# Two half heads of attention probabilities turned by VectorE blocks and a DRAM round trip, and the sample rows' averaging later in the order

## The chip, the cores and the metric

The kernel runs on one core of a Trainium2 chip. It has five engines with a queue of instructions each: PE (TensorE, matrix products and transposes), DVE (VectorE), ACT (ScalarE), POOL (GpSimd) and SP (SyncE, which here only issues DMAs). The metric is the device time of one execution in microseconds (us), the median over the runs.

## The reference

One layer of a hybrid decoder, for a prompt of 512 tokens and 8 running sequences with one new token each (the sample rows), d_model 1024, in float32. What this case touches is mixer B, the dilated window attention of the prompt, and the layer norm of the sample rows at the end:

```
for window, dil in ((128, 1), (512, 4), (2048, 16)):       # mixer B, 8 heads of 64
    dist = arange(window // dil + 1) * dil;  idx = q_idx[:, None] - dist     # rows < 0 are masked
    logits = einsum('bqhd,bqjhd->bhqj', q, k[idx]) * 64**-0.5 + rel_bias[t5_bucket(dist)].T
    m = max(logits);  p = exp(logits - m);  s = sum(p)
    outs += [einsum('bhqj,bqjhd->bhqd', p, v[idx]) / s]
o_b = sum(w * o) / sum(w),  w = s * exp(m - max over the three m)
...
mix = concat([o_a * silu(ga), o_b * silu(gb)])             # o_a: gated linear attention, 4 heads
y = mix @ w_out                                            # 1024 x 1024
x_new = layer_norm(2**0.25 * x + y, ln_g, ln_b)            # for the prompt's and for the sample rows
```

## The kernel before

All work of the step is one program for one core. The input projection goes by column groups (`ps_qa`, `ps_ka`, `ps_qb`, ... are PSUM tiles of these groups); matrices are split into a high and a low part (`hi_`, `lo_`), and each product is the sum of three matmuls. Then come both mixers, and at the end the output projection: `ps_y` matmuls by row pairs of the prompt, whose result VectorE adds to `y`, followed by the layer norm.

**The order of the work.** Every stage is a generator, a task, that yields one instruction after another. A planner (class `Plan`) issues them: the table `TIMES` (L241) has a due time for each step of each task, and the planner always takes the task whose next step is due first (`run`). Each engine executes its instructions in the order in which they were issued, so the table sets the order on every engine; the times in it are not waits. A trailing `a` in the table picks the second of two engines where a step offers two (VectorE or ScalarE). All instructions are recorded under the one line that issues them, L677 (L679 in the changed kernel). `QUEUE` says for each round trip through DRAM which engine issues its DMAs: `G` is POOL, `D` is SyncE.

**Softmax and values of the prompt.** The queries come in four blocks of 128, two to a half (`pi` 0 and 1). `softmax(h, q, ...)` (L1650) takes the scores of head `h` and block `q` from PSUM, adds the bias strip, takes the exponential (ScalarE) and the sum, and normalises into `pr`. The keys that are far away are folded in a tile `far`. The rest of `pr` is turned: TensorE transposes its 128x128 blocks into a bank `ps_pt`, and VectorE or ScalarE copies them into `pt`, which holds two heads (tile `pt21` is the second half of heads 4 and 5). `weighted(g, pi)` (L1696) waits for four heads and multiplies `far` and `pt` by the values `vp` and `v` into `ps_pv`, as one batch of matmuls, first all of `far`, then `pt` by heads. `weighted(1, 1)` takes the second half of heads 4 to 7.

**Turning through DRAM.** Other tiles are turned in another way already. `blocks` (L1046) transposes inside each 32x32 block on VectorE, `store_blocks` (L1051) writes the result to a scratch tensor in DRAM, and `load_turned` (L1055) reads it back with the blocks exchanged, in pieces of 32 numbers, 128 bytes. `ysc` and `yx` are such a pair for a part of the output, `vsc` for values, `osc` for mixer A.

**The sample rows at the end.** `residual_sample` (L2209) turns the sample rows' output (`ps_ys`), adds it to `w_s`, sums over the row (`sums_s`), averages over the row's parts by a small matmul with a matrix `avg` into `ps_ms` (the mean), subtracts, squares, and averages again into `ps_vs` (the variance):

```
        yield V.tensor_reduce(sums[:, 0:1], y, axis=AX.X, op=ALU.add)
        ps = yield bank("t", "ps_ms")
        yield T.matmul(ps[:ROWS, 0:1], avg, sums_s[:, 0:1], start=True, stop=True)
        yield V.tensor_copy(sums[:, 0:1], ps[:64, 0:1])
```

These small matmuls stand on TensorE in the middle of the `ps_y` matmuls of the output projection. `early_mean` and `last_norm` finish the last row pair. SyncE issues nearly all DMAs in one order: weights, the cached keys (`past`) and values (`vv`, each with its factors `pb`) of the eight running sequences, the bias strips, and the stores.

Of the kernel before, what the change touches and what calls it, by code (L numbers as in the profile page):

```python
# [21 lines left out]
P = 128  # L22
# [58 lines left out]
QUEUE = dict(y="G", v="D", k="G", o="D", a="D")  # L81
SLOW, SHARE = 1100, 1.7

# [159 lines left out]
first_loads 302 1 1 1 1 1 1 1 1225 2286 187 794 1 1 1 1 1 1 1 1 1 1 10481 3044 1  # L243
# [36 lines left out]
softmax|0|0|ps_s00|pr00 71199 352 723 534a 940 514  # L280
softmax|0|1|ps_s00|pr00 71401 533a 745 449 1793 109 494a
softmax|1|0|ps_s10|pr10 71736 689 659 455 3680 286a
sample_logit|0|past0|qbc0 71782 167 1786 6 1787 1980
# [16 lines left out]
evac_f|ps_vb0_f1|1 83824a 2706 -191 588 8171  # L300
# [18 lines left out]
sample_softmax 103293 726 338a 3854 19 473 80 1533 3 8495 4537 119 119 97 553 136 1206 475 400 292 -77 1473 1161 80263  # L319
keys_out|ps_kb3_1|3|1 103292  # L320
keys_store|1 105547 1358 1 1303 1 1940 159 8
sample_logit|7|past7|qbc7 110333 4933 1 2304 1239 1586
evac|ps_gb0_0|0 106220 693 17 1176a 104
evac|ps_gb0_1|1 108107 1 1 1
evac_f|ps_vb1_f0|0 118480a 439a 9948
values_store|0 117568
evac_f|ps_vb1_f1|1 115262a 6000a 3961 1 8209
values_turn|0 117569 1 1239 2
sample_v|vnt|vnt|out_7_dram 117565 1a 1
# [4 lines left out]
evac|ps_gb1_0|0 129481 642 617 872 78  # L334
scores|1|1 124376 397
# [15 lines left out]
softmax|5|0|ps_s50|pr50 134486 1252 896 64a 6389 6
softmax|5|1|ps_s50|pr50 134834 1383 483 427a 7587 1 670a
weighted|0|1 136602 2460a 1250a
softmax|6|0|ps_s60|pr60 140937 392 657 608a 2788 5a
softmax|6|1|ps_s60|pr60 143973 1 333 1 3333 405 341a
softmax|7|0|ps_s70|pr70 144973 1 2463 547a 1685 335a
evac_f|ps_va0_f1|1 144565a 47a 584 1126 6000 599
values_store|1 146916
softmax|7|1|ps_s70|pr70 146915 725 1213 354a 867 776 695a
mix_b|1|0 149500 500 1500  # L360
mix_b|1|1 151500 500 1500
evac|ps_va0_2|2 149776
values_turn|1 156714 986 1100 979
sample_value|2|vv2|pb2 157706 359 738 1975 2787
evac|ps_va0_3|3 151292a
scores|2|1 150934 1089
softmax|5|2|ps_s52|pr52 154303 952 1152 1752a 2622 2104 1869 1 5a
# [3 lines left out]
softmax|5|3|ps_s53|pr53 154696 1263 753 1641 4028 733 1642 1a 4a  # L371
sample_value|3|vv3|pb3 164764 974 1104 519 4664
evac|ps_gb2_0|0 156601 109 643 338 4
evac|ps_gb2_1|1 158795 6 975 1001
scores|3|1 164789 1
softmax|6|2|ps_s62|pr62 165736 1619 1519 494a 682 521 2064 798 232
sample_value|4|vv4|pb4 175659 3 1724 613 3989
softmax|6|3|ps_s63|pr63 166837 1902 793 190 1063 299 4436 1 1a
softmax|7|2|ps_s72|pr72 165733 1100 525 249a 2540 249 38 138 391
evac_f|ps_va1_f0|0 165732 1 411 3 886a  # L380
softmax|7|3|ps_s73|pr73 167352 2344 699 690a 8 2024 1707 1 371a
sample_value|5|vv5|pb5 184671 1 10 1 5285
# [12 lines left out]
sample_value|7|vv7|pb7 195635 1 4315 111 3631
gla_head|0|0 188890 1 240 242 534 1 2628a 245a 265a 590a
gla_head|0|1 191991 1 1 1 2528 72 4128a 1a 1a 490a
evac|ps_gb3_1|1 185463
mix_b|1|3 199537 4796 1
evac|ps_ga0_0|0 193940 250  # L400
# [281 lines left out]
def trunk(ctx: ExitStack, tc: tile.TileContext, xT, xp, xs, state, ck, cv, w_in, wab, gnorm,  # L682
# [95 lines left out]
    B = {}  # L778
# [1634 lines left out]
```

## Time and profile before

| | |
|---|---|
| runs shown | 274.9, 276.59, 277.6 us; median 276.59 |
| profiled execution, its own time | 273.72 us |
| its span | 271.9 us |
| TensorE, matmul | 262.8 us busy, 97% |
| VectorE | 217.6 us, 80% |
| ScalarE | 152.5 us, 56% |
| POOL | 72.9 us, 27% |
| the queue of SyncE's DMAs | 75.9% of 16 DMA engines' time, 56.69 MB |

The span goes from the first to the last instruction of the profiled execution; what lies around it makes the rest of its own time. Busy shares are averages over the whole span; the stages have different limits, so what an edit is worth is read at its own place. An engine named in brackets behind a row is what ended the idle time before that row.

### The profile page before, as it was taken

How to read it: one execution, taken by the hardware profiler on the slowest of the kernel's cores; microseconds unless marked ns; L12 is line 12 of the kernel's file. 1: busy time of each engine (PE TensorE's matmuls, PEld its weight loads, DVE VectorE, ACT ScalarE, POOL GpSimd, SP SyncE). 2: the span in 40 equal slices, each digit the busy share in tenths (PEclk: the TensorE clock that was granted, in tenths of full speed). 3: DMA queues.
4: the chain of work that ended last, by engine and by line, in shares of the span. 5: the costliest groups of instructions: out<-in, count | busy, mean ns of one | idle time of the engine just before them, and what ended most of it. 6: DMA issues, size and time to landing. Idle time of an engine off the chain costs nothing.

```text
span 271.9 us, 7336 instructions
## 1 busy us (share of the span) xinstructions
PE 262.8 (97%) x2831; PEld 246.2 (91%) x2831; DVE 217.6 (80%) x542; ACT 152.5 (56%) x450; POOL 72.9 (27%) x92
## 2 busy tenths in 40 slices
PE   8999999999999999999999999999999999997990
PEld 4999999999999999999989899989999999985890
DVE  4753889999999999486985888976798996429895
ACT  4754766665647393436874785654859456104511
POOL 3000000000263945810054153454753001420200
PEclk9999999999999999999999999999999999997997
DMA  7995698255998899959999996998799899993132
GB/s 221 348 250 120 170 284 232 69 136 161 309 304 174 273 272 216 241 158 272 278 188 283 318 199 192 287 308 257 231 216 236 233 230 259 314 206 83 77 154 82
DMA packets 79215, 60.10 MB, mean 221 GB/s; under 512 B 28453, under 2 KB 69995, under 8 KB 79181
## 3 DMA queue, kind: packets, MB, share of 16 engines
q1 hardware_dynamic: 77981, 56.69, 75.9%
q0 software_dynamic: 768, 2.62, 4.1%
q8 instruction: 22, 0.36, 0.6%
q10 hardware_dynamic: 432, 0.33, 0.4%
q14 instruction: 12, 0.10, 0.1%
HBM read 49.62 MB, written 10.80 MB: 222 GB/s over the span
## 4 chain that ended last, share of the span: by engine, by line
PE 69%; DVE 12%; DMA 11%; ACT 4%; issue 2%; SPq 1%; DVEq 0%; ACTq 0%; POOLq 0%
PE ps_qb L677 9%; PE ps_kb L677 9%; PE ps_gb L677 7%; PE ps_y L677 6%; PE ps_ka L677 5%; PE ps_vb_f L677 4%; PE ps_vb L677 4%; PE ps_qa L677 4%; PE ps_ga L677 4%; DMA y<-in_xp_dram 4%; DMA yx<-ysc 3%; PE ps_va L677 2%; PE ps_pv L677 2%; PE ps_va_f L677 2%; PE ps_l L677 2%; DMA vv<-in_cv_dram 2%
## 5 line engine op out<-in xcount | busy, mean ns | idle before, releaser
L677 POOL TENSOR_TENSOR past<-past,qbc 128x256 f32<-128x256 f32 x32 | 26.3, 854 | 80.6 <-DMA qbc<-qsd 73.9
L677 POOL TENSOR_TENSOR vv<-vv,pb 128x256 f32<-128x256 f32 x32 | 26.9, 872 | 51.9 <-DMA pb<-psd_s 27.9
L677 ACT ACTIVATE pr<-pr,ms 128x128 f32<-128x128 f32 (+3 forms) x52 | 24.7, 492 | 14.7 <-DVE ms L677 14.6
L677 PE MATMUL ps_ka<-xx,hi_ka 128*128 128x264 f32 (+1 forms) x64 | 12.7, 294 | 0.1
L677 DVE CUSTOM_DVE_ANT_0 pr<-ps_s,strip 128x128 f32<-128x128 f32 (+3 forms) x32 | 11.9, 407 | 0.8 <-DMA strip<-tabx 0.5
L677 ACT ACTIVATE d<-d 128x512 f32<-128x512 f32 x11 | 6.8, 643 | 10.0 <-DVE d L677 10.0
L677 ACT COPY pt<-ps_pt 128x256 f32<-128x256 f32 (+1 forms) x23 | 7.6, 348 | 8.3 <-PE ps_pt L677 8.3
L677 PE MATMUL ps_pt<-cf,pr 128*128 128x128 f32 x56 | 11.0, 278 | 0.1
L677 PEld LDWEIGHTS ps_ka<-xx,hi_ka 128*128 128x128 f32 x64 | 10.2, 197 | 0.9 <-ACT hi_ka L677 0.9
L677 DVE TENSOR_REDUCE lt<-past 128x8 f32<-128x512 f32 x16 | 10.4, 672 | 0.0
L677 DVE TENSOR_REDUCE o_pv<-vv 128x4 f32<-128x1024 f32 x8 | 9.7, 1206 | 0.0
L677 POOL DMA_DIRECT2D ysc<-yw x3 | 2.3, 782 | 25.3 <-DVE yw L677 25.3
L677 PE MATMUL ps_ka<-xx,lo_ka 128*128 128x264 f32 (+1 forms) x32 | 8.9, 291 | 0.0
L677 DVE SCALAR_TENSOR_TENSOR y<-y,yx 128x256 f32<-128x256 f32 x6 | 2.4, 414 | 7.7 <-DMA yx<-ysc 7.7
L677 PEld LDWEIGHTS ps_pt<-cf,pr 128*128 128x128 f32 x56 | 6.6, 140 | 1.1 <-ACT pr L677 0.5
L677 ACT ACTIVATE qh<-ps_qb 128x128 fp32r<-128x128 f32 x16 | 5.2, 436 | 3.3 <-PE ps_qb L677 3.3
L677 PE MATMUL ps_pv<-pt,v 128*64 128x128 f32 (+1 forms) x80 | 6.9, 318 | 0.0
L677 PE MATMUL ps_s<-kp,qh 64*128 64x256 f32 (+1 forms) x64 | 6.8, 302 | 0.0
L677 DVE TENSOR_TENSOR d<-b 128x1024 f32<-128x1024 f32 (+1 forms) x6 | 6.8, 1130 | 0.0
L677 DVE RECIPROCAL ms<-ms 128x1 f32<-128x1 f32 x32 | 4.4, 153 | 2.8 <-ACT pr L677 2.7
L677 DVE STREAM_TRANSPOSE yw<-feat_y 128x256 f32<-128x256 f32 x6 | 3.6, 626 | 3.7 <-ACT feat_y L677 3.7
L677 ACT COPY feat_y<-ps_yf 128x256 f32<-128x256 f32 x8 | 2.9, 368 | 6.5 <-PE ps_yf L677 6.5
(566 smaller groups left out, 1075.0 us busy)
## 6 DMA issues: line engine op xcount, KB each, us to landing
past<-in_ck_dram SPq DMA_DIRECT2D x8, 512.0 KB, 5.4
vv<-in_cv_dram SPq DMA_DIRECT2D x8, 512.0 KB, 7.0
pb<-psd_s SPq DMA_DIRECT2D x8, 512.0 KB, 9.0
s<-in_state_dram SPq DMA_DIRECT2D x4, 512.0 KB, 5.5
qbc<-qsd SPq DMA_DIRECT2D x8, 256.0 KB, 4.7
y<-in_xp_dram SPq DMA_DIRECT2D x4, 512.0 KB, 3.5
x_raw<-in_xT_dram SPq DMA_DIRECT2D x6, 260.0 KB, 5.6
out_dram<-y SPq DMA_DIRECT2D x3, 512.0 KB, 2.6
```

Source lines behind the costliest of these rows:

```text
L677: getattr(eng.eng, op.fn)(*op.args, **op.kw)
```

## The change

Three things change.

First, a list `BY_DRAM` names two halves of heads: head 0 first half, head 5 second half. Their `pr` is turned by VectorE's 32x32 block transposes straight into `pt`, and when both query blocks of the half are there, the tile is stored into a scratch tensor `psc` in DRAM (192 KB for head 0, 256 KB for head 5) and loaded back into the same place, turned (1536 and 2048 pieces of 128 bytes). Both DMAs are issued by SyncE. Seven TensorE transposes (three of head 0, four of head 5) and their four copies out of PSUM are left out; four block transposes, two stores and two loads are new.

Second, `residual_sample` gets later due times from its `sums_s` on.

Third, the rest of the table of due times is written anew in many places, so that neighbours change places on all engines but POOL, whose order stays as it was. Among these, four ScalarE steps `s<-s,a_s` stand earlier.

```diff
-QUEUE = dict(y="G", v="D", k="G", o="D", a="D")
+QUEUE = dict(y="G", v="D", k="G", o="D", a="D", p="D")
+BY_DRAM = [(0, 0), (5, 1)]
...
-softmax|5|2|ps_s52|pr52 154303 952 1152 1752a 2622 2104 1869 1 5a
-softmax|5|3|ps_s53|pr53 154696 1263 753 1641 4028 733 1642 1a 4a
+softmax|5|2|ps_s52|pr52 154303 952 1152 1752a 2622 2104 218
+softmax|5|3|ps_s53|pr53 154696 1263 753 1641 4028 733 335 530 6430
...
-residual_sample 214696 1 840 507 26537 906 2067 2101 343 181 346 2398 1 1 1364 10028 717 353
+residual_sample 214696 1 840 507 26537 2919 1500 5000 200 200 600 4000 300 300 300 3600 1000 400
...
+    psc = {(h, pi): scratch(f"psc{h}{pi}", 3 + pi) for h, pi in BY_DRAM}
...
+        nk = (n - far) // P
+        if (h, pi) in BY_DRAM:
+            w = B[f"pt{h // 2}{pi}"][:, h % 2, :(3 + pi) * P].rearrange("p (k q) -> p k q", q=P)
+            yield blocks(w[:, j * (1 + pi):j * (1 + pi) + nk], pr[:, far:n])
+            free(pr_all)
+            mark(f"pw{h}{pi}")
+            if plan.marks[f"pw{h}{pi}"] == 2:
+                yield store_blocks(queue["p"], psc[h, pi], w)
+                yield load_turned(queue["p"], w.rearrange("p k (a j) -> p (k a) j", j=32), psc[h, pi])
+                for _ in range(2):
+                    mark(f"p{h}{pi}")
+            return
         pt = yield bank("t", f"ps_pt{h}{q}")
-        nk = (n - far) // P
         for k in range(nk):
             yield T.transpose(pt[:, k * P:k * P + P], pr[:, far + k * P:far + k * P + P], ident)
```

Three places in the order. On TensorE the mean of the sample rows, before (`mhb`, `mlb` are parts of the mixed features of mixer B, `mha`, `mla` of mixer A, `hi_wo` and `lo_wo` the output weights; numbers are buffer numbers):

```order
L677 MATMUL ps_y_3981<-hi_wo__3499,mla_3662 128x512
L677 MATMUL ps_y_4030<-hi_wo__3551,mhb_2138 128x512
L677 MATMUL ps_y_4030<-lo_wo__3552,mhb_2138 128x512
L677 MATMUL ps_y_4030<-hi_wo__3551,mlb_2139 128x512
L677 MATMUL ps_ms<-sums_s,avg 66x1
L677 MATMUL ps_y_4030<-hi_wo__3551,mhb_2138 128x512
L677 MATMUL ps_y_4030<-lo_wo__3552,mhb_2138 128x512
```

and in the changed kernel:

```order
L679 MATMUL ps_y_4025<-hi_wo__3726,mha_3660 128x512
L679 MATMUL ps_y_4025<-lo_wo__3727,mha_3660 128x512
L679 MATMUL ps_y_4025<-hi_wo__3726,mla_3661 128x512
L679 MATMUL ps_ms<-sums_s,avg 66x1
L679 MATMUL ps_y_4025<-hi_wo__3726,mha_3660 128x512
L679 MATMUL ps_y_4025<-lo_wo__3727,mha_3660 128x512
L679 MATMUL ps_y_4025<-hi_wo__3726,mla_3661 128x512
L679 MATMUL ps_y_4086<-hi_wo__3549,mhb_2134 128x512
```

Before, three matmuls of this `ps_y` tile stood ahead of `ps_ms`, now all but the last three do: `ps_ms` has moved 18 matmuls later, and `ps_vs`, which was 16 instructions behind it, now stands 23 behind.

On SyncE the stretch of the fifth and sixth `vv` (buffers `vv4`, `vv5`), before, with the semaphores that each DMA waits for (DMAHW are earlier DMAs of the ring):

```order
L677 DMA vv4_2778<-in_cv_dram 128x1024 [waits DMAHW0_49,Pool_49]
L677 DMA pb4_2853<-psd_s_95 128x1x1024 [waits DMAHW1_49,DVE_49]
L677 DMA raw0_ga2__2870<-in_w_in_dram 128x8x128 [waits DMAHW2_49,Activation_49]
L677 DMA raw0_ga3__2883<-in_w_in_dram 128x8x128 [waits DMAHW3_49,Activation_49]
L677 DMA vv5_2928<-in_cv_dram 128x1024 [waits DMAHW4_49,Pool_49]
L677 DMA pb5_2963<-psd_s_95 128x1x1024 [waits DMAHW5_49,DVE_49]
```

and in the changed kernel:

```order
L679 DMA vv4_2778<-in_cv_dram 128x1024 [waits DMAHW2_49,Pool_49]
L679 DMA psc51_104<-pt21_2756 128x4x128 [waits DMAHW3_49,DVE_49]
L679 DMA pb4_2847<-psd_s_95 128x1x1024 [waits DMAHW4_49,DVE_49]
L679 DMA raw0_ga2__2864<-in_w_in_dram 128x8x128 [waits DMAHW5_49,Activation_49]
L679 DMA raw0_ga3__2877<-in_w_in_dram 128x8x128 [waits DMAHW6_49,Activation_49]
L679 DMA vv5_2922<-in_cv_dram 128x1024 [waits DMAHW7_49,Pool_49]
L679 DMA pt21_2756<-psc51_104 128x16x32 [waits DMAHW3_49,DMAHW0_49,PE_49]
L679 DMA pb5_2958<-psd_s_95 128x1x1024 [waits DMAHW1_49,DVE_49]
```

Head 5's store has come between `vv4` and `pb4`, and its load between `vv5` and `pb5`. Head 0's store and load stand much earlier on SyncE, the load right ahead of the store `vsc<-vbw` of the first values.

On ScalarE the squares of the second `ps_oa` (mixer A's output; `s` is the running state of the sequences), before:

```order
L677 CAST hi_wo__3450<-raw_wo__3292 128x512 x2
L677 ACTIVATE sq,ssq<-ps_oa_3397 128x128
L677 ACTIVATE sq,ssq<-ps_oa_3398 128x128
L677 ACTIVATE sq,ssq<-ps_oa_3397 128x128
L677 ACTIVATE sq,ssq<-ps_oa_3398 128x128
L677 ACTIVATE s_3269<-s_3269,a_s 128x128 x4
L677 ACTIVATE sq,ssq<-ps_oa_3397 128x128
```

and in the changed kernel:

```order
L679 ACTIVATE oa_3029<-ps_oa_3163,rmss 128x128
L679 ACTIVATE s_3264<-s_3264,a_s 128x128 x4
L679 CAST hi_wo__3450<-raw_wo__3284 128x512 x2
L679 ACTIVATE sq,ssq<-ps_oa_3397 128x128
L679 ACTIVATE sq,ssq<-ps_oa_3398 128x128
```

The four `s<-s,a_s` stood in the middle of the squares and now stand ahead of them and of the two casts. On VectorE, head 5's two block transposes stand ahead of the reduction `o_pv<-vv` and of the copy `feat<-ps_va_f`.

More of the change, by code (lines that the diff above doesn't have):

```diff
@@ L279 @@
 keys_out|ps_kb0_1|0|1 73438
-softmax|0|0|ps_s00|pr00 71199 352 723 534a 940 514
-softmax|0|1|ps_s00|pr00 71401 533a 745 449 1793 109 494a
+softmax|0|0|ps_s00|pr00 70260 352 723 534a 802
+softmax|0|1|ps_s00|pr00 71401 533a 745 449a 6000 1435 5055
 softmax|1|0|ps_s10|pr10 71736 689 659 455 3680 286a
-sample_logit|0|past0|qbc0 71782 167 1786 6 1787 1980
+sample_logit|0|past0|qbc0 71778 1 1 1 3747 1980
 softmax|1|1|ps_s10|pr10 71938 1191 602 8 3763 1 6a
@@ L318 @@
 evac|ps_kb3_1|1 103284 7
-sample_softmax 103293 726 338a 3854 19 473 80 1533 3 8495 4537 119 119 97 553 136 1206 475 400 292 -77 1473 1161 80263
 keys_out|ps_kb3_1|3|1 103292
-keys_store|1 105547 1358 1 1303 1 1940 159 8
-sample_logit|7|past7|qbc7 110333 4933 1 2304 1239 1586
+sample_softmax 107106 1 1a 1101 21 473 80 1533 3 8495 4389 267 119 97 553 136 1206 475 400 292 -77 1473 1161 81937
+sample_logit|5|past5|qbc5 98500 3187 1 1 3857 1388
 evac|ps_gb0_0|0 106220 693 17 1176a 104
+keys_store|1 106424 481 1 1303 1 1940 159 8
 evac|ps_gb0_1|1 108107 1 1 1
+sample_logit|6|past6|qbc6 110190 1 16 1 7240 1
+sample_logit|7|past7|qbc7 110333 4933 1 2304 1443 1382
 evac_f|ps_vb1_f0|0 118480a 439a 9948
+evac_f|ps_vb1_f1|1 118479a 6000a 3961 1 8209
+sample_v|vnt|vnt|out_7_dram 117565 1a 1
 values_store|0 117568
-evac_f|ps_vb1_f1|1 115262a 6000a 3961 1 8209
 values_turn|0 117569 1 1239 2
-sample_v|vnt|vnt|out_7_dram 117565 1a 1
 evac|ps_vb1_2|2 118812a
@@ L333 @@
 sample_values 126150 4645 -308 1121 10667 2825 3358 717 13578 2296 5229 2031 8031 2620 6193 2570
-evac|ps_gb1_0|0 129481 642 617 872 78
-scores|1|1 124376 397
+evac|ps_gb1_0|0 130591 642 617 872 78
+scores|1|1 123466 397
+mix_b|0|0 125209 646 10841
+mix_b|0|1 131386 1660 2329
 softmax|2|2|ps_s22|pr22 126804 562 961 514 641 474 780 1 531
@@ L356 @@
 softmax|7|0|ps_s70|pr70 144973 1 2463 547a 1685 335a
+softmax|7|1|ps_s70|pr70 146915 725 1213 354a 867 776 695a
 evac_f|ps_va0_f1|1 144565a 47a 584 1126 6000 599
-values_store|1 146916
-softmax|7|1|ps_s70|pr70 146915 725 1213 354a 867 776 695a
 mix_b|1|0 149500 500 1500
 mix_b|1|1 151500 500 1500
+values_store|1 146916
+values_turn|1 156714 986 1100 979
 evac|ps_va0_2|2 149776
-values_turn|1 156714 986 1100 979
 sample_value|2|vv2|pb2 157706 359 738 1975 2787
+scores|2|1 150934 1089
 evac|ps_va0_3|3 151292a
-scores|2|1 150934 1089
-softmax|5|2|ps_s52|pr52 154303 952 1152 1752a 2622 2104 1869 1 5a
+sample_value|3|vv3|pb3 161850 3888 1104 519 4664a
 softmax|4|2|ps_s42|pr42 152536 287 1 224 7724 1 1 1 335
@@ L392 @@
+evac|ps_va1_3|3 178179a
 evac|ps_gb3_0|0 183537 208
 mix_b|0|3 186087 485 1175
+evac|ps_gb3_1|1 185463
 gla_out|0 187351
+gla_head|0|0 188890 1 240 242 534 1 3758a 1a 1a 1a
+mix_b|1|3 199537 4796 1
 sample_value|7|vv7|pb7 195635 1 4315 111 3631
[L396 to L400, printed above, removed]
+gla_head|0|1 191856 1 1 1 2528 72 4128a 1a 1a 490a
+evac|ps_ga0_0|0 193465 1
@@ L401 @@
+evac|ps_ga0_1|1 196731
 mix_a|0|0 193600 1000 4400 17600 1358 489 884 1142
+evac|ps_ga1_0|0 198891 1
 mix_sample_b 211242 1 3967 1 7
-evac|ps_ga0_1|1 196731
-gla_out|1 200808
-mix_a|0|1 198799 1 5835 12196 1231 443 1391 585
+gla_out|1 202402
+mix_a|0|1 198799 1 5835 10585 2842 443 1391 585
+evac|ps_ga1_1|1 204606
 gla_head|1|0 200986 1 1 1 1 1 6939a 114 4a 263
-gla_head|1|1 203431 1 1 1 1 5647 18a 1 1a 1
-evac|ps_ga1_0|0 198698 1
+gla_head|1|1 203431 1 1 1 1 5462 1a 1 203a 1
+evac|ps_ga2_0|0 207591 314
@@ L420 @@
-out_turn|0|0|ps_yf00 225620a 1a 1929
+out_turn|0|0|ps_yf00 224722a 1a 1
 out_turn|0|1|ps_yf01 228116a 254a 366 561 6118
@@ L428 @@
 residual|3 237549
-out_turn|3|1|ps_yf31 241977a 2a 1560 1
 out_evac|0|0|yx0 238537 1155
@@ L432 @@
 ln_rows 239209 1
+out_turn|3|1|ps_yf31 240091a 1888a 1560 1
 out_evac|0|3|ps_yt3 243797 1604
@@ L440 @@
 norm|0 248945 213 1 638 224 238 2646 531
-norm|1 250277 1 1 1 1 1216 2053 1249
+norm|1 247493 1 1 1 1 1216 2053 1249
+centre 251716
+centre# 257218
 out_evac|2|2|ps_y22 250877
-centre 251716
 norm|2 253857 1605 531 560 713 1 333 491 1353 1290
-centre# 256320
 out_evac|3|2|ps_y32 258848 1784 480
+seed_sum|y3 259965 1660
 centre## 257599
 early_mean|3|ps_y31 261513 588 465 11 275 201 1 388 328 1 908
-seed_sum|y3 260719 1660
 last_norm|3|ps_y30 264326 565 30 69 396 190 189 471 1 661 1 514
```

72 lines of the change are left out of this document (32 added, 40 removed).

## The prediction

> **What bounds the kernel now.** I read the first page of the profile, then the waits of TensorE, then stretch by stretch the timelines of TensorE and VectorE, and last the DMA issues on SyncE's queue. From the page and from the waits (engine, what it waited for: us in total, times, longest):
>
> ```profile
> span 271.9 us, 7336 instructions
> PE 262.8 (97%) x2831; PEld 246.2 (91%) x2831; DVE 217.6 (80%) x542; ACT 152.5 (56%) x450; POOL 72.9 (27%) x92
> PE 69%; DVE 12%; DMA 11%; ACT 4%; issue 2%; SPq 1%; DVEq 0%; ACTq 0%; POOLq 0%
> ...
> PE ps_ms L677 <- DVE sums_s L677: 1.7, 1, 1.7
> PE warm_ps L677 <- PEq L2401: 0.8, 1, 0.8
> ```
>
> TensorE is busy for 97% of the span and is the chain for 69% of it, and after its start it waits once in the whole program: for `ps_ms`, the mean of the sample rows. So there is little idle time on TensorE to win but this, and anything that makes TensorE wait anew costs its length. The place of that wait (start, duration, idle time before it in brackets; then windows with busy times, and the granted clock as the third number from the end):
>
> ```profile
> 244.93 0.40 PE L677 MATMUL ps_y<-hi_wo__3551,mlb 128*128 128x512 f32 x1
> 246.99 0.28 PE L677 MATMUL ps_ms<-sums_s,avg 66*66 66x1 f32 x2 [1.66 <-DVE sums_s L677]
> 248.14 0.40 PE L677 MATMUL ps_y<-lo_wo__3619,mhb 128*128 128x512 f32 x1
> 248.38 0.42 PE L677 MATMUL ps_y<-hi_wo__3618,mlb 128*128 128x512 f32 x1
> 249.02 0.63 PE L677 MATMUL ps_y<-lo_wo__3619,mhb 128*128 128x512 f32 x1
> 251.58 0.61 PE L677 MATMUL ps_y<-lo_wo__3678,mha 128*128 128x512 f32 x1
> ...
> 248.60:252.00 3.40, 3.40 (x9) 2.61 (x8) 2.36 (x9) 3.21 (x10) 0.00 (x0) 0.50 0.00 0
> 252.10:255.00 2.90, 2.90 (x16) 2.31 (x15) 2.32 (x4) 0.65 (x3) 1.72 (x2) 1.00 0.00 0
> ```
>
> The wait is 1.66 us. Then the clock is 0.50 for 3.4 us: the six steps from 249.02 to 251.58 take 0.43 us each, where 248.14 to 248.38 took 0.24. Half of 3.4 us is lost, 1.7 us. Wait and slow stretch together cost TensorE 3.3 to 3.4 us.
>
> TensorE is not alone at the end. The timelines of VectorE, with a row each of ScalarE and POOL behind it:
>
> ```profile
> 243.22 0.76 DVE L677 SCALAR_TENSOR_TENSOR y<-y,yx 128x256 f32<-128x256 f32 x2 [7.73 <-DMA yx<-ysc]
> 246.68 0.26 DVE L677 TENSOR_REDUCE sums_s<-w_s 64x1 f32<-64x128 f32 x1
> 252.52 0.15 DVE L677 COPY sums_s<-ps_vs 64x1 f32<-64x1 f32 x1 [1.42 <-PE ps_vs L677]
> 254.02 0.69 DVE L677 SCALAR_TENSOR_TENSOR y<-y,ps_y 128x512 f32<-128x512 f32 x1 [0.16 <-PE ps_y L677]
> 262.59 0.42 DVE L677 SCALAR_TENSOR_TENSOR y<-y,ps_y 128x256 f32<-128x256 f32 x1
> 265.45 0.47 ACT L677 ACTIVATE sq_y<-ps_y,tail 128x256 f32<-128x256 f32 x1 [5.37 <-PE ps_y L677]
> 236.12 3.45 POOL L677 DMA_DIRECT2D yx<-ysc  x3 [1.39 <-DMA y<-in_xp_dram]
> ```
>
> From 243.22, when `yx` (a part of the output that comes back turned from DRAM) has landed, to 262.59, the step that begins the last row pair, VectorE has 19.4 us with only 1.42 + 0.16 of waiting in it: 17.8 us of work in a row, released by a DMA.
>
> **Part 1: the averaging of the sample rows stands later.** `ps_ms` comes 18 of the large `ps_y` matmuls later on TensorE. At 0.24 each that is 4.3 us, more than the 1.66 that it waited, so the wait goes, and with it, as I take it, the slow clock: TensorE gets up to 3.4 us ahead. The time doesn't follow by that much, because VectorE is late next. Its 17.8 us of work still begin when `yx` lands; all it can lose are its own two waits, 1.42 + 0.16 = 1.6 us. `ps_vs` too stands later, behind so many matmuls that VectorE has its other work to do before it reads it. After 262.59 the chain goes on with VectorE, ScalarE and `ps_y` (ScalarE's wait at 265.45), all of which are 1.6 us earlier if TensorE is. Part 1 gives 1.6 us; the bounds are 0 (if the wait only moves to `ps_vs`) and 3.4 (if VectorE had slack).
>
> The Trainium skill, "TensorE: Matmul & The Clock Gate", Part 1 and "Why this matters for your kernels", has the clock fall to half after an idle window of some 3.4 us and asks for no idle gaps beyond about 3 us. By that rule the 1.66 us here would have cost no clock, and part 1 would save TensorE 1.7 instead of 3.4; the row at 248.60 differs from it (0.50 after a gap of 1.66 us), and the measurement decides.
>
> **Part 2: transposes off TensorE, blocks onto VectorE.** Seven transposes of 128x128 leave TensorE and four copies out of PSUM leave ScalarE (three) and VectorE (one); four block transposes come to VectorE. The timelines of TensorE and VectorE where head 5's stand, and two groups of block transposes (busy, mean ns of one):
>
> ```profile
> 164.99 0.60 PE L677 MATMUL ps_pt<-cf,pr 128*128 128x128 f32 x4
> 165.52 0.50 PE L677 MATMUL ps_s<-kp,qh 64*128 64x256 f32 x4
> 167.38 0.38 PE L677 MATMUL ps_turn<-cf,feat 128*128 128x128 f32 x2
> ...
> 164.97 1.21 DVE L677 TENSOR_REDUCE o_pv<-vv 128x4 f32<-128x1024 f32 x1
> 166.18 0.41 DVE L677 COPY feat<-ps_va_f 128x256 f32<-128x256 f32 x1
> ...
> L677 DVE STREAM_TRANSPOSE kw<-ps_kb 128x256 f32<-128x256 f32 x8 | 3.4, 431 | 0.0
> L677 DVE STREAM_TRANSPOSE yw<-feat_y 128x256 f32<-128x256 f32 x6 | 3.6, 626 | 3.7 <-ACT feat_y L677 3.7
> ```
>
> Four transposes take 165.52 - 164.99 = 0.53 us, so seven save 0.93 us on TensorE. A block transpose of 128x256 takes 0.43 to 0.63 us. Of head 5 two stand on VectorE ahead of `o_pv` and `feat`: 0.9 to 1.25 us. `feat` ended at 166.59 and TensorE's `ps_turn` at 167.38 reads it, 0.8 us of slack; TensorE now comes there 0.53 earlier, so `feat` at 167.5 to 167.85 holds it up until 0.1 to 0.45 after its old time. Head 5's 0.53 is lost there, with up to 0.45 more; head 0's 0.4 may stay (its blocks stand among VectorE work of a stage in which TensorE waits for nothing). Bounds -0.9 to +0.5; I take 0. The copies' leaving ScalarE (56% busy) is worth nothing.
>
> **Part 3: the way through DRAM.** Both heads' store and load are issued by SyncE. Its timeline, TensorE's at `ps_pv`, the DMA issues of two short windows and of one at 207 (KB each, us to landing), and the summary of the loads `v<-vsc`, which like the new ones come back in pieces of 128 bytes:
>
> ```profile
> 88.82 0.39 SPq L677 DMA_DIRECT2D vsc<-vbw  x1
> 118.12 1.52 PE L677 MATMUL ps_pv<-pt,v 128*64 128x256 f32 x16
> 166.26 0.49 SPq L677 DMA_DIRECT2D vv<-in_cv_dram  x1
> 169.52 4.01 SPq L677 DMA_DIRECT2D vv<-in_cv_dram  x1
> 174.02 0.59 SPq L677 DMA_DIRECT2D pb<-psd_s  x1
> 177.79 1.52 PE L677 MATMUL ps_pv<-far,vp 128*64 128x256 f32 x16
> 179.14 1.91 PE L677 MATMUL ps_pv<-pt,v 128*64 128x128 f32 x24
> ...
> vv<-in_cv_dram SPq DMA_DIRECT2D x1, 512.0 KB, 5.5
> ...
> vv<-in_cv_dram SPq DMA_DIRECT2D x1, 512.0 KB, 9.8
> ...
> ow<-osc SPq DMA_DIRECT2D x1, 256.0 KB, 3.3
> ...
> 135.34 7.04 SPq L677 DMA_DIRECT2D raw_va__2326<-in_w_in_dram  x1
> DMA to landing us min/median/max: 3.8/6.3/8.7
> 203.32 1.16 ACT s L677 x4
> ```
>
> Head 0's load stands in the order right ahead of the store `vsc<-vbw`, issued at 88.82, and the first `ps_pv` out of `pt` runs at 118.12: 29 us of cover, more than three times the longest landing in these rows, so it costs TensorE nothing. Head 5's store goes behind the fifth `vv`, its load behind the sixth. The fifth `vv` landed at 166.26 + 5.5 = 171.8, the sixth at 169.52 + 9.8 = 179.3 with four transfers of 512 KB in that time: 1.9 us per 512 KB, one after the other. The new store (256 KB) puts 0.94 ahead of the sixth `vv`, and the new load's own 256 KB come behind it: 179.3 + 0.94 + 0.94 = 181.2. TensorE's `ps_pv` needs it at about 179.2, as the second group of matmuls out of `pt`. So TensorE waits 2.0 us, a wait that the kernel did not have. Bounds: no wait (the load as `ow<-osc` at 207, 256 KB in 3.3 us: issued behind the sixth `vv`, at about 174.4, it lands at 177.7), and 4.8 us (the load as the slower `v<-vsc`, also of 128-byte pieces, 8.7 us, and the store's 0.9 ahead: 184.0). I take 2.0, since the rows of this very stretch have the queue served in order.
>
> What does the wait cost at the end? TensorE may be 3.4 late until the tail without being the bound: 2.0 passes there. But the wait shifts everything that leads to `yx`: `ps_oa`, ScalarE's squares, VectorE's turns, POOL's DMA. One item gives back: four `s<-s,a_s` on ScalarE, 1.16 us on the chain of waits at 203.32, stand earlier in the order and leave that chain (its row is the last of the fence). `yx` lands 2.0 - 1.2 = 0.8 later, and of part 1's 1.6 us 0.8 is left.
>
> The Trainium skill, "DMA: Bandwidth & Descriptors", Anatomy of one DMA, has about 2.0 us and bytes by 436 GB/s; for 256 KB my estimate from it is 2.6 us. By it the load would land at 177.0 and the wait would not be there; the row of 9.8 us in this stretch differs from it, and I go by that row.
>
> **Base.** The profiled execution took 273.72 us, 1.8 more than its span; the runs' median is 276.59 (274.9 to 277.6). I subtract differences from the median: 276.59 - 0.8 = 275.8 (272.9 against the profiled run). One per cent is 2.8 us, about what a measurement of this kernel can tell from no change: faster is under 273.8, slower over 279.4.
>
> **The rivals.**
> - *Forecast (0.36).* Wait of 2.0, no slow clock after it: 275.8; between 275.0 (a saved transpose or `yx` held by the loads of `y` and not by the chain) and 276.6.
> - *No wait at head 5 (0.32).* The load lands by 179. For it: `ow<-osc`'s 3.3 us; against it: 9.8 us for the sixth `vv`. Then 1.6 stay; of the 1.2 from ScalarE half, 0.6, as `yx` was issued behind the loads of `y` (POOL's 1.39 wait); and half of the 0.93: 2.7 us, 273.9.
> - *The wait brings its own slow clock (0.16).* As after 1.66 us at 245. TensorE is 2.0 + 1.7 = 3.7 late, `yx` 2.5: 1.6 - 2.5 is 0.9 slower, 277.5.
> - *The load is the new bound (0.16), the other side.* The 2048 pieces of 128 bytes land at 184.0; the wait is 4.8, with 1.7 of slow clock 6.5; 6.5 - 1.2 = 5.3 on `yx`, less 1.6: 3.7 slower, 280.3. For it: `v<-vsc` took up to 8.7 us, and the issue right behind it on SyncE took 7.04 where others take 0.5. It turns slower than before from a wait of 2.8 without slow clock (2.8 - 1.2 = 1.6), and slower by over 1% from 5.6 us of lateness in all.
>
> **How the numbers follow.** Faster by over 1%: half of the second case, 0.16, and 0.06 from the forecast if VectorE had slack that I don't see: 0.22. Slower by over 1%: 0.13 of the fourth case and 0.03 of the third: 0.16. The rest is 0.62. The range goes from 273.2, two thirds into the second case, to 278.8, past the third case and into the fourth; it leaves out about 0.1 on each side. The forecast's own range is 275.0 to 276.6.
>
> **What would show it.** In the profile after: no wait at `ps_ms`, granted clock 1.00 in the tail, no wait of VectorE at `ps_vs` (part 1); `ps_turn` behind `feat` by under half a us (part 2); a wait of TensorE at `ps_pv` for the DMA into `pt` of about 2 us near 179 (part 3), and VectorE's work from `yx` to the last row pair at 17.8 us in one piece. I am wrong if `ps_pv` doesn't wait at all, if it waits over 3 us, if the clock falls behind it, or if VectorE has idle time between `yx` and the last pair.

## The result, and the profile after

The changed kernel took 278.98 us (median; 278.15 to 279.3), the kernel before beside it 275.75 us: a ratio of 1.0132, with a 95% interval of 1.0089 to 1.0176. In a second comparison the ratio was 1.0126 (1.0056 to 1.0195). The change makes the kernel 1.3% slower, 3.6 us. The forecast was 0.8 us faster, with a range up to 278.8. A ratio leaves out runs that lie over 1.5% above the fastest one of their kernel, so a ratio and two medians need not agree to the last tenth.

The page and TensorE's waits in the changed kernel:

```profile
span 276.9 us, 7325 instructions
PE 261.5 (94%) x2824; PEld 244.7 (88%) x2824; DVE 223.0 (81%) x544; ACT 152.1 (55%) x448; POOL 74.7 (27%) x92
PE 48%; DVE 21%; DMA 17%; ACT 5%; issue 5%; SPq 2%; POOL 0%; DVEq 0%; POOLq 0%
...
PE ps_kb L679 <- DVE ms L679: 1.4, 1, 1.4
PE ps_yf L679 <- DVE mlb L679: 1.3, 1, 1.3
PE ps_pt L679 <- ACT pt L679: 1.1, 1, 1.1
PE warm_ps L679 <- PEq L2415: 0.8, 1, 0.8
PE ps_turn L679 <- DVE feat L679: 0.6, 1, 0.6
PE ps_pt L679 <- ACT pr L679: 0.4, 1, 0.4
PE ps_og L679 <- issue: 0.2, 1, 0.2
PE ps_pv L679 <- DMA pt<-psc: 0.2, 1, 0.2
```

TensorE has 1.3 us less work, but its one wait at `ps_ms` has become six others, and its share of the chain fell from 69% to 48%, while VectorE's and the DMAs' rose from 12 and 11 to 21 and 17. (`warm_ps` is the start; "issue" is idle time in which TensorE waited for nothing that the profile shows.) The tail, in the timelines of TensorE and VectorE and in two windows (the granted clock is the third number from the end):

```profile
254.51 0.23 PE L679 MATMUL ps_ms<-sums_s,avg 66*66 66x1 f32 x2
259.79 0.23 PE L679 MATMUL ps_vs<-sums_s,avg 66*66 66x1 f32 x2
...
248.60:252.00 3.40, 3.40 (x17) 2.74 (x16) 1.41 (x5) 0.00 (x0) 0.00 (x0) 1.00 1.02 186
252.10:255.00 2.90, 2.90 (x16) 2.31 (x15) 2.90 (x10) 0.00 (x0) 0.00 (x0) 1.00 0.49 144
...
247.71 0.76 DVE L679 SCALAR_TENSOR_TENSOR y<-y,yx 128x256 f32<-128x256 f32 x2 [5.94 <-DMA yx<-ysc]
251.70 0.42 DVE L679 SCALAR_TENSOR_TENSOR y<-y,yx 128x256 f32<-128x256 f32 x1 [1.99 <-DMA yx<-ysc]
263.31 0.14 DVE L679 COPY sums_s<-ps_vs 64x1 f32<-64x1 f32 x1
267.61 0.40 DVE L679 SCALAR_TENSOR_TENSOR y<-y,ps_y 128x256 f32<-128x256 f32 x1
```

Part 1 did what it says: `ps_ms` and `ps_vs` don't wait, the clock is 1.00, VectorE no longer waits at `ps_vs`. What is worse is ahead of it: the first turned output lands 4.5 us later than before (247.71 for 243.22), and the second, which came in time before, now holds VectorE up again until 251.70.

Four places on the way there: SyncE around head 5's load, two stretches of the chain of waits (the chain that the profile follows back from the last instruction), POOL, and the VectorE step `o_pv`.

```profile
172.32 3.86 SPq L679 DMA_DIRECT2D vv<-in_cv_dram  x1
176.29 0.38 SPq L679 DMA_DIRECT2D pt<-psc  x1
177.39 3.80 SPq L679 DMA_DIRECT2D pb<-psd_s  x1
185.48 0.55 SPq L679 DMA_DIRECT2D pb<-psd_s  x1
...
176.29 6.46 DMA pt<-psc
182.79 1.95 PE ps_pv L679 x20
...
206.01 1.30 ACT sq L679 x10
207.32 6.60 DMA raw_wo__3390<-in_w_out_dram
...
186.35 2.84 POOL L679 TENSOR_TENSOR vv<-vv,pb 128x256 f32<-128x256 f32 x4 [4.44 <-DMA pb<-psd_s]
194.02 4.26 POOL L679 TENSOR_TENSOR vv<-vv,pb 128x256 f32<-128x256 f32 x4 [4.83 <-DMA pb<-psd_s]
198.37 0.52 POOL L679 TENSOR_SCALAR ssq<-ssq 128x4 f32<-128x4 f32 x1
198.97 1.02 POOL L679 TENSOR_TENSOR rmss<-ssq,less_half 128x4 f32<-128x4 f32 x1
...
184.24 1.21 DVE L679 TENSOR_REDUCE o_pv<-vv 128x4 f32<-128x1024 f32 x1
```

The same steps of POOL, SyncE and VectorE before:

```profile
188.57 2.84 POOL L677 TENSOR_TENSOR vv<-vv,pb 128x256 f32<-128x256 f32 x4 [3.61 <-DMA pb<-psd_s]
191.49 1.05 POOL L677 TENSOR_SCALAR ssq<-ssq 128x4 f32<-128x4 f32 x1
192.62 1.34 POOL L677 TENSOR_TENSOR rmss<-ssq,less_half 128x4 f32<-128x4 f32 x1
...
182.37 0.55 SPq L677 DMA_DIRECT2D pb<-psd_s  x1
...
181.13 1.21 DVE L677 TENSOR_REDUCE o_pv<-vv 128x4 f32<-128x1024 f32 x1
```

The load `pb` behind head 5's load takes 3.80 us to issue, where it took 0.59 before (the row at 174.02); it is through 4.5 us after head 5's load is (181.19 and 176.67). POOL then gets its factors `pb` later each time, and the step in its queue behind them, `ssq` and `rmss` (the norm of mixer A, which has nothing to do with these factors), starts 6.9 us later than before.

It would be easy to join the two, and the rows don't allow it. The `pb` that `ssq` stands behind is not the load right behind head 5's but the next one, issued at 185.48. In this trace, in the one before and in those of all experiments, it is issued 0.02 to 0.03 us after VectorE's `o_pv` has ended (185.45 here, 182.34 before), so SyncE is not what holds it back. The 6.9 us are 3.1 of `o_pv`'s lateness, 2.3 of a longer way from issue to POOL's step (8.5 for 6.2 us), and 1.4 of a longer POOL step (4.26 for 2.84). TensorE is as late as `o_pv` then: its `ps_pv` out of `far` starts 3.1 us later than before (180.90 for 177.79).

Nor does the chain of this execution go over POOL. It goes from head 5's load over `ps_pv`, where the wait is only 0.2 us, along TensorE to ScalarE's squares of the second `ps_oa` (`sq`), then over a load of output weights (`raw_wo`), for which ScalarE waits 1.9 us, to the turns through `osc` and `ysc` and to `yx`. In a second trace of the changed kernel (e14, below) the chain does go over the `pb` at VectorE's `o_pv`, `ssq` and `rmss`. So the two traces of the same kernel put the loss on two different paths.

### The profile page after: what moved, and what is told of

Its sections match the earlier page's. It is cut to its first block, busy times and chain, and to the rows that moved or that the text cites. A ratio compares the mean times of both kernels' runs of the same rounds, so it can differ in the third digit from the quotient of the medians.

```text
span 276.9 us, 7325 instructions
## 1 busy us (share of the span) xinstructions
PE 261.5 (94%) x2824; PEld 244.7 (88%) x2824; DVE 223.0 (81%) x544; ACT 152.1 (55%) x448; POOL 74.7 (27%) x92
## 4 chain that ended last, share of the span: by engine, by line
PE 48%; DVE 21%; DMA 17%; ACT 5%; issue 5%; SPq 2%; POOL 0%; DVEq 0%; POOLq 0%
PE ps_qb L679 9%; PE ps_gb L679 6%; PE ps_kb L679 5%; PE ps_qa L679 5%; PE ps_ka L679 4%; DVE y L679 4%; PE ps_ga L679 4%; DMA pb<-psd_s 4%; DMA yx<-ysc 3%; DMA raw_wo__3390<-in_w_out_dram 2%; DMA ysc<-yw 2%; DMA pt<-psc 2%; DVE pr L679 2%; PE ps_vb_f L679 2%; PE ps_vb L679 2%
## 5 line engine op out<-in xcount | busy, mean ns | idle before, releaser
L679 POOL TENSOR_TENSOR past<-past,qbc 128x256 f32<-128x256 f32 x32 | 27.2, 882 | 80.9 <-DMA qbc<-qsd 76.0
L679 POOL TENSOR_TENSOR vv<-vv,pb 128x256 f32<-128x256 f32 x32 | 28.6, 924 | 56.1 <-DMA pb<-psd_s 32.5
L679 ACT ACTIVATE pr<-pr,ms 128x128 f32<-128x128 f32 (+3 forms) x53 | 25.3, 495 | 22.1 <-DVE ms L679 22.1
L679 PE MATMUL ps_pt<-cf,pr 128*128 128x128 f32 x49 | 9.8, 279 | 1.5 <-ACT pt L679 1.1
L679 ACT COPY pt<-ps_pt 128x256 f32<-128x256 f32 (+1 forms) x20 | 6.6, 341 | 4.5 <-PE ps_pt L679 4.4
L679 PEld LDWEIGHTS ps_pt<-cf,pr 128*128 128x128 f32 x49 | 5.9, 140 | 2.6 <-ACT pt L679 1.3
L679 PE MATMUL ps_kb<-xx,hi_kb__1224 128*128 128x264 f32 (+1 forms) x32 | 5.9, 285 | 1.4 <-DVE ms L679 1.4
L679 ACT ACTIVATE rstd<-mv,ln_eps 128x1 f32<-128x1 f32 x3 | 0.9, 290 | 11.0 <-DVE mv L679 11.0
L679 ACT ACTIVATE s<-s,a_s 128x128 f32<-128x128 f32 x16 | 5.6, 418 | 2.4 <-DMA s<-in_state_dram 2.4
```

The costliest lines, as they stand in the source:

```text
L679: getattr(eng.eng, op.fn)(*op.args, **op.kw)
```

## The experiments

The medians, with the ratio to the kernel before and its interval. "Table" is the new due times without the averaging's, "averaging" `residual_sample`'s.

| run | what it has | median | ratio (95%) |
|---|---|---|---|
| e3_resid_only | averaging | 274.41 | 0.9977 (0.9935 to 1.0019) |
| e1_table_only | table, averaging | 274.55 | 1.0016 (0.9976 to 1.0056) |
| e10_new_no_trip | table, averaging, blocks | 275.45 | 1.0031 (0.9986 to 1.0076) |
| e11_big_pieces | all, both loads in 512 bytes | 276.11 | 1.0055 (1.0014 to 1.0095) |
| e15_big_h5 | all, head 5's load in 512 bytes | 276.17 | 1.0075 (1.0037 to 1.0112) |
| e16_big_h0 | all, head 0's load in 512 bytes | 278.58 | 1.0170 (1.0120 to 1.0219) |
| e14_changed_again | all | 277.70 | 1.0126 (1.0056 to 1.0195) |
| e4_only_h0 | all but head 5's part | 275.94 | 1.0062 (1.0025 to 1.0100) |
| e5_only_h5 | all but head 0's part | 275.78 | 1.0025 (0.9970 to 1.0079) |
| e2_dram_only | DRAM parts | 280.33 | 1.0145 (1.0054 to 1.0235) |
| e7_no_trip | blocks alone | 274.69 | 0.9996 (0.9938 to 1.0054) |
| e8_old_h5 | head 5's part | 278.45 | 1.0001 (0.9945 to 1.0058) |
| e9_old_h0 | head 0's part | 275.90 | 1.0013 (0.9964 to 1.0062) |
| e12_dram_and_resid | DRAM parts, averaging | 277.24 | 1.0064 (1.0010 to 1.0118) |
| e13_ln_rows_later | averaging, gamma and beta later | 273.10 | 0.9890 (0.9812 to 0.9967) |
| e17_ln_rows_again | the same | 271.22 | 0.9913 (0.9869 to 0.9957) |

### The parts, one by one

My theory after the two traces was that the way through DRAM costs the time, by SyncE's queue; its rival that the rewritten table does.

e1, the changed kernel with no half through DRAM:

```diff
-BY_DRAM = [(0, 0), (5, 1)]
+BY_DRAM = []
 (softmax|0|0, 0|1, 5|2, 5|3: the old due times)
```

> The changed kernel with the list of halves through DRAM empty and the old due times for the four softmax tasks concerned; the rest of the new table stays, the later averaging too. Theory Q (the way through DRAM costs: 2048 pieces on SyncE's queue hold up the loads behind them, POOL and then the turned output): 1.5 to 3.5 us faster than before, no wait of TensorE over 1 us between 90 and 170, yx landing earlier than before or at most 1 us later. Rival T (the rewritten table costs, since TensorE's waits at 95 and 145 in the changed kernel come from neighbours that changed places): 1 to 3 us slower than before, the waits of 1.5 and 1.4 us there still.

e2, the kernel before with the new code and the four softmax tasks' new due times; e3, the kernel before with one new line:

```diff
-residual_sample 214696 1 840 507 26537 906 2067 2101 ...
+residual_sample 214696 1 840 507 26537 2919 1500 5000 ...
```

> The kernel before with both halves through DRAM and the new due times of their four softmax tasks alone; the averaging of the sample rows stays where it was. Theory Q: 4 to 7 us slower than before (yx 6 to 8 us later, SyncE's load behind the one into pt takes 3 to 4 us to issue), the wait at ps_ms and the half clock behind it possibly gone because yx is late. Rival T: within 1.5 us of before.

> The kernel before with the new due times of the sample rows' averaging alone. The prediction's part 1: 1.6 us faster, no wait at ps_ms, clock 1.00 at 248 to 252, no wait of VectorE at ps_vs. If VectorE had room that the prediction did not see, up to 3.5 us faster (the changed kernel took 25.2 us from yx landing to the end, before 28.7). If the wait only moves on: 0.

e5, the changed kernel with `BY_DRAM = [(5, 1)]` and the old due times for head 0's two tasks:

> The changed kernel with head 5's half alone through DRAM and head 0's four copies and transposes as before. Theory Q: nearly all of the loss is here, 2 to 4 us slower than before. Rival T: as the changed kernel (3.6 slower), and so is the kernel without any half through DRAM. If head 0 carries the loss: 1 to 3 us faster than before.

The table with the averaging costs nothing that can be measured (1.0016), the DRAM parts alone, block transposes included, cost as much as the whole change (1.0145): this points at the way through DRAM. The rival is not empty, though. The two waits that it named are there without any DRAM, in e1:

```profile
PE ps_pt L679 <- ACT pt L679: 1.4, 1, 1.4
PE ps_kb L679 <- DVE ms L679: 1.3, 1, 1.3
```

They are the table's, and may be what takes back the averaging's gain: e1 lies 0.4% above e3, though the two intervals overlap. In e1's trace `yx` comes 2.6 us later than in the kernel before (245.81 for 243.22), with no half through DRAM. e3's gain is 0.6 us by its ratio (1.8 faster to 0.5 slower). In e3's trace `yx` came 1.8 us later than in the kernel before, and yet the span is the same (272.0 and 271.9):

```profile
245.02 0.76 DVE L677 SCALAR_TENSOR_TENSOR y<-y,yx 128x256 f32<-128x256 f32 x2 [8.76 <-DMA yx<-ysc]
```

From that step to the end it is 27.0 us, before 28.7: the tail is 1.7 us shorter. Nothing that stands ahead of `yx` differs between these two kernels; its 1.8 us is what one execution differs from the next.

e5 was a surprise: head 5's half alone, in the new table, came out at 1.0025, where I had 2 to 4 us slower.

### Head 0 or head 5, blocks or DRAM

> The changed kernel with head 0's half alone through DRAM, head 5's as before. With head 5's half alone the time was +0.7 us (-0.8 to +2.2), with none +0.4, with both +3.6. Theory H0 (head 0's load carries the loss: its 1536 pieces stand ahead of the first values and of the sample keys on SyncE): 2.5 to 3.5 us slower than before. Theory H5 (head 5's load carries it, the run with it alone was a lucky draw): within 1 us of before. Theory B (each costs little, together they add up): 1 to 2 us slower.

e7 leaves out the two stores and loads, so that the two halves come out turned only inside their 32x32 blocks:

```diff
-                yield store_blocks(queue["p"], psc[h, pi], w)
-                yield load_turned(queue["p"], w.rearrange(...), psc[h, pi])
```

> The kernel before with the two halves turned by VectorE's 32x32 blocks as in the run with DRAM alone (4.0 us slower), but the two stores and two loads left out, so that the blocks of these two halves stay at their old places. Theory DMA (the two stores and loads on SyncE's queue cost the 4 us): between 0.5 faster and 1 slower than before. Theory V (VectorE's four block transposes cost it, ahead of what TensorE and POOL wait for: TensorE waits 1.5 at ps_turn): 2 to 4 us slower.

> The kernel before with head 5's half alone through DRAM (with its two tasks' new due times). Theory H5: 3 to 4 us slower than before, yx 3 us or more later. Theory H0: within 1 us. Theory B: 1.5 to 2.5 slower.

> The kernel before with head 0's half alone through DRAM (with its two tasks' new due times). Theory H5: within 0.8 us of before. Theory H0: 2.5 to 4 us slower. Theory B: 1.5 to 2.5 slower.

e7 is at 0.9996: VectorE's block transposes alone cost nothing that can be measured in the old order, which leaves the DMAs. Neither theory on the heads held as it was put: head 0 alone stands at 0.6% with the new table, which has 0.2% without it, and costs nothing that can be measured in the old one. Head 5 alone in the old table is the kernel with the widest runs, 273.75 to 283.15: its median is 3.1 us up and its ratio, which takes in three of its ten runs, 1.00. Whether head 5's half costs anything there is left open by this. The trace is of a run of 278.43 us; from TensorE's timeline and two windows:

```profile
180.89 1.53 PE L679 MATMUL ps_pv<-pt,v 128*64 128x128 f32 x11 [2.15 <-DMA pt<-psc]
...
178.00:181.30 3.30, 1.15 (x19) 0.90 (x17) 2.85 (x8) 0.41 (x2) 1.10 (x3) 1.00 0.57 119
181.40:184.70 3.30, 3.30 (x30) 2.40 (x30) 0.95 (x1) 0.54 (x2) 0.87 (x2) 0.50 0.85 209
```

In this execution the prediction's step stands as it was put: TensorE waits 2.15 us for head 5's load (forecast 2.0), and half clock follows it for 3.4 us, the third case of the prediction.

### Bytes or pieces

e10 leaves the stores and loads out of the changed kernel; the two halves come out as in e7. e11 keeps them and loads the same bytes without exchanging the blocks, in pieces of 512 bytes:

```diff
-                yield load_turned(queue["p"], w.rearrange("p k (a j) -> p (k a) j", j=32), psc[h, pi])
+                sc = psc[h, pi]
+                yield queue["p"].dma_start(w, bass.AP(tensor=sc.tensor, offset=sc.offset, ap=[[P, P], [P * P, 3 + pi], [1, P]]))
```

> The changed kernel with the two stores and two loads left out; the blocks of the two halves stay at their old places, all else (table, block transposes, averaging later) is the changed kernel's. Theory DMA (the two ways through DRAM cost the time, TensorE's waits at 95 and 145 belong to the table and are cheap): 0.5 to 1.5 us faster than before, as without any half through DRAM. Rival (block transposes and order cost it together): 2 us or more slower than before.

> The changed kernel with both loads in pieces of 512 bytes (384 and 512 of them) in place of 128 bytes (1536 and 2048): same bytes, same places in the order, but the blocks come back unexchanged. Theory P (the number of pieces costs: the load behind takes 3.8 us to issue, all later loads are that much later): 0 to 1.5 us slower than before. Rival L (the extra 0.9 MB and the loads' waiting in the queue cost it): 3 to 4 us slower, as the changed kernel.

> The kernel before with both halves through DRAM and the averaging of the sample rows later, the rest of the table old. If the loss of DRAM alone (5 us in the mean of its runs) is a longer wait at ps_ms with two half clocks behind it, moving the averaging takes that away: 1 to 2.5 us slower than before. If it is the late yx alone, the averaging gives its 1.3 and 3.5 to 4 are left.

e12 was 1.8 us slower in the median, 3.1 us less than e2: by the medians the averaging takes away much of what the DRAM parts cost in the old order, though the intervals of the two ratios overlap. In e2 TensorE waited 4.9 us at `ps_ms`; that wait, and 6.8 us of half clock behind it, are in the trace of e2, a run of 279.1 us.

e10 stands at 1.0031 and e11 at 1.0055: with the same bytes in bigger pieces more than half of the loss is gone. e14, e15 and e16 put the changed kernel beside one with big pieces for head 5 alone and one for head 0 alone (the same edit, under a condition on the head):

> The changed kernel itself once more, beside the next two on the same chip, since it has four runs only. Theory P (pieces of 128 bytes cost 2.8 of its 3.6 us): 3 to 4 us slower than before, and slower than both kernels below by 1 us or more, at least than one of them. If its four runs were an unlucky draw: 0.5 to 1.5 slower, as with pieces of 512 bytes.

> The changed kernel with head 5's load alone in pieces of 512 bytes (512 of them), head 0's in 1536 pieces of 128. If head 5's pieces carry the loss (SyncE's next load takes 4 us to issue there, POOL gets its factors late, then the norm of mixer A): 0 to 1.5 slower than before. If head 0's: 3 to 4 slower. If both add up: about 2.

> The changed kernel with head 0's load alone in pieces of 512 bytes (384 of them), head 5's in 2048 pieces of 128. If head 5's pieces carry the loss: 3 to 4 slower than before. If head 0's: 0 to 1.5. If both add up: about 2.

Where head 0's half goes through DRAM too, head 5's pieces carry more than half of the loss: with its 2048 small pieces 1.0126 and 1.0170, with 512 big ones 1.0055 and 1.0075. Head 0's pieces make no difference that could be measured; of the two with small pieces for head 5 only e16's interval lies clear of the other two. SyncE and POOL with big pieces for head 5 (e15):

```profile
175.35 0.38 SPq L679 DMA_DIRECT2D pt<-psc  x1
176.19 0.58 SPq L679 DMA_DIRECT2D pb<-psd_s  x1
...
191.02 2.83 POOL L679 TENSOR_TENSOR vv<-vv,pb 128x256 f32<-128x256 f32 x4 [4.05 <-DMA pb<-psd_s]
193.94 1.15 POOL L679 TENSOR_SCALAR ssq<-ssq 128x4 f32<-128x4 f32 x1
195.17 1.34 POOL L679 TENSOR_TENSOR rmss<-ssq,less_half 128x4 f32<-128x4 f32 x1
```

The load behind is issued in 0.58 us, 1.0 us after head 5's, and POOL's `ssq` starts 4.4 us earlier than in the changed kernel. Against the second trace of the changed kernel (e14, the first row below) it is 2.6 us, and with no store and no load at all (e10, the second) `ssq` starts later than in e15:

```profile
196.53 0.52 POOL L679 TENSOR_SCALAR ssq<-ssq 128x4 f32<-128x4 f32 x1
...
195.65 1.11 POOL L679 TENSOR_SCALAR ssq<-ssq 128x4 f32<-128x4 f32 x1
```

What stays open is, first, e5: it has head 5's small pieces and no loss by its ratio, with runs from 273.81 to 279.62. Its trace shows the same 4-us issue and a late `ssq`, so whether the loss needs head 0's part too isn't settled.

Second, the way by which the small pieces cost time. A late `ssq` is not their mark: with head 0's half alone (e4), so without any DMA for head 5, it starts at 197.28, later than in e14. Nor is a late `yx`: it comes 3.2 us later than before in e10 and in e15, 3.9 in e11, and with small pieces 4.5 in the changed kernel, 3.9 in its second trace and 5.7 in e16. Most of its lateness is there without the small pieces, then, and the rest is hard to tell from the 1.8 us by which one execution differs from the next (e3). The times show what the pieces cost; the traces don't show on which path.

### A version that beats both

The traces put the end down to `yx`'s landing plus VectorE's tail. In the kernel before, two loads that nobody needs before 252 are issued around the first `yx` and share its way:

```profile
235.57 0.33 SPq L677 DMA_DIRECT2D gamma<-in_ln_g_dram  x1
236.86 0.33 SPq L677 DMA_DIRECT2D beta<-in_ln_b_dram  x1
```

e13 is e3 with these two behind the state's store on SyncE, and e17 the same once more:

```diff
-ln_rows 239209 1
+ln_rows 242000 1
```

> The kernel before with the averaging later and, beside it, the loads of gamma and beta (512 KB each) behind the state's store on SyncE, so that the turned output yx does not queue behind them. If yx's landing sets VectorE's tail and is late by these bytes: yx 2 to 3.5 us earlier, 3 to 4.5 us faster than before. If yx is held by the loads of y: as the averaging alone, 1.3 faster in the mean. If gamma is now late for the first norm: slower than that.

> The kernel before with the averaging later and gamma and beta behind the state's store, once more and in more rounds, since it has four runs only: 2 to 3 us faster than before if those four stand for it, and 1 us or more faster than the averaging alone (1.3 in its mean); 1.3 if gamma and beta do nothing.

It took 271.22 us, a ratio of 0.9913 (0.9869 to 0.9957), and in the first comparison 0.9890: 1% faster than the kernel before. Its SyncE, VectorE and the summary of the tile `yx`:

```profile
242.75 0.53 SPq L677 DMA_DIRECT2D gamma<-in_ln_g_dram  x1
240.56 0.76 DVE L677 SCALAR_TENSOR_TENSOR y<-y,yx 128x256 f32<-128x256 f32 x2 [5.89 <-DMA yx<-ysc]
DMA to landing us min/median/max: 4.8/5.1/5.3
```

`yx` lands 4.8 to 5.3 us after its issue, before 7.1 to 7.8, and VectorE's tail starts 2.7 us earlier. By the two ratios the later loads give 1.8 us on top of the averaging alone (e3, 0.9977); the intervals of the two just overlap, so this part is less sure than the whole. In this trace gamma lands at 248.26 and its first use starts at 248.28: it could not come later.

## Why the prediction was wrong

**Part 1, 1.6 us faster: right in mechanism, and its size is not contradicted.** The wait, the slow clock and VectorE's waits went, and VectorE was what came next: TensorE's last matmul started 2.6 us earlier in e3 (262.53 for 265.14), and the span stayed the same. The tail got 1.7 us shorter, the kernel 0.6 by the ratio, and its interval holds 1.6 as well as no gain. What the step took too simply is the slow clock behind `ps_ms`, as if it came with every such wait (below).

**Part 2, nothing: not contradicted, its wait mis-sized.** e10 above e1 is 0.15%, 0.4 us, inside the bounds of -0.9 and +0.5, though each of the two ratios is known to some 1.2 us only. The wait at `ps_turn` for `feat` that it named is there, but where it had 0.1 to 0.45 us, the two traces of the changed kernel have 0.6 and 1.6, and e10 has 1.5.

**The rest of the table, 1.2 us given back: wrong.** The prediction looked for what the new due times move on the path of its three parts and found the four `s<-s,a_s`. The two places where they make TensorE wait, `ps_kb` behind VectorE's scores at 95 and `ps_pt` at 145, it did not look at. It put these at nothing, without a reason. In e1 they are 2.7 us of TensorE, and `yx` is 2.6 us later. The earlier `s<-s,a_s` did shorten ScalarE's squares of the second `ps_oa`, from 3.3 us to 2.2; but these start 3.8 us later, since TensorE does (206.01 for 202.18), so `yx` gains nothing.

**Part 3, this is the step that failed: "But the wait shifts everything that leads to `yx`" and "`yx` lands 2.0 - 1.2 = 0.8 later".** The prediction gave the way through DRAM one price, TensorE's wait at `ps_pv` for head 5's load. The load's landing was well read: forecast 181.2, in the changed kernel 182.75. But TensorE came there 3.1 us late itself and waited 0.2 us; in e14 it didn't wait at all, one of the prediction's own signs of being wrong; in e8 it waited 2.15. Still `yx` was 4.5 us later in the changed kernel and 3.9 in e14.

Two things stand in the place of that price. One is the rest of the table, above: without the DMAs `yx` is 2.6 (e1) to 3.2 us (e10) later already, though by their ratios these two kernels cost only 0.4 and 0.9 us, which lies inside their intervals. The other is the number of pieces, to which the prediction gave no price beyond the landing of `pt`: with head 5's 2048 pieces the ratio is 1.0126 to 1.0170, with 512 pieces of the same bytes 1.0055 to 1.0075, so some 2 us of the loss of 3.6. What the pieces do at their place is plain: SyncE got its next load out 4.5 us after them. The prediction had quoted a row of this kind (7.04 us for the load behind `v<-vsc`), and followed it only for the landing of `pt`. How the 4.5 us there become some 2 us at the end stays open.

The prediction's estimate of 2.6 us, which it set aside, rests on a fit that the Trainium skill, "DMA: Bandwidth & Descriptors", Anatomy of one DMA, gives for DMAs that GpSimd issues. This load was issued by SyncE, behind other loads of its queue, and took 6.46 us.

**The rivals.** The fourth, slower by 3.7, had the sign and half of the cause: the small pieces and SyncE. That its size fits too is luck: its price ran over a TensorE wait of 4.8 us with slow clock, and that wait was 0.2. The third, a half clock behind the new wait, happened in e8. The second, no wait at head 5, is nearly what the changed kernel's `ps_pv` shows, at 2.7 us faster: no wait there, and slower all the same. The four cases shared two assumptions: that a late load matters through the engine that reads it, and that the rest of the table makes TensorE wait nowhere.

## What to carry to other kernels

Here a DMA in 2048 small pieces held up the DMA behind it on its queue by some 4 us, so price a DMA also by the next few loads behind it and by the engines that wait for them. Before a path is written down, check at each step what released it: two late steps in a row need not be cause and effect. Before a new wait is priced, the whole order is to be read for places where two engines meet within some tenths of a microsecond, not only the lines that the change speaks of. Where the end hangs on a landing, look for transfers beside it that nobody needs yet.

## What the runs showed of the hardware

**The clock falls after less idle time than three microseconds, and by chance of its place.** The record of the granted clock in the traces has half rate in stretches of 3.41 us, or whole multiples, on a grid of 3.41 us that starts at another time in each execution. Across the 18 traces, while TensorE had work, the half clock followed where TensorE stood idle for 1.66 us or more inside one such stretch (1.66 before, 1.93 in two pieces in e5, 1.94 in e9, 2.15 and 2.17 in e8, 2.17 and, in the stretch behind it, 2.70 in e2), and did not where it was 1.63 (e14) or less. In e7 the wait at `ps_ms` was longer than before, but a boundary of the grid, at 246.8, cut it into 0.92 and 0.85, and the clock stayed full:

```profile
247.63 0.28 PE L679 MATMUL ps_ms<-sums_s,avg 66*66 66x1 f32 x2 [1.77 <-DVE sums_s L679]
...
246.90:250.20 3.30, 2.57 (x13) 2.12 (x14) 3.30 (x12) 0.99 (x3) 0.00 (x0) 1.00 0.44 127
```

The Trainium skill, "TensorE: Matmul & The Clock Gate", Part 1, has the window of 3413 ns that runs freely, with which the grid agrees; that a whole window must be idle does not agree with the 1.66 us. One half-rate stretch in a span of 272 us lowers its mean clock by about 0.006 and, at half speed, costs TensorE 1.7 us. That fits the runs of the kernel before: 22 with a granted clock of 0.992 or more took 273.7 us in the mean, 53 with 0.985 to 0.989 took 275.2. Other delays, which bring the idle time, may have their part in this step; the runs don't part them from the clock.

**2048 pieces of 128 bytes hold the issuing queue.** The load behind them was through 4.5 us after them in the changed kernel, and 4.2 to 4.5 us in the six other traces with these pieces, whether the time lay in the issue itself (3.80 in the changed kernel, 4.40 in e12) or partly ahead of it (e16: 2.08); behind 512 pieces of 512 bytes with the same bytes it was 1.0 (e15). The load of small pieces was not slower itself: it took 6.46 us to landing, with big pieces 6.46 (e15).
